# A fused two-block kernel: sums of layer 0's modulation, the end of its MLP, and block 2's second layer rearranged

## The chip, the cores and the metric

One core of one Trainium2 chip runs the whole program, a single launch. The metric is device microseconds (us), the median of the runs shown. TensorE (PE) multiplies, VectorE (DVE) and ScalarE (ACT) work on rows and evict PSUM, GpSimd (POOL) makes small powers, memsets and issues some DMAs, SyncE (SP) issues the weight loads. Every engine, and every engine's DMA queue, takes its instructions in one fixed order.

## What is computed

Block 1 is a gated residual block on 256 tokens of width 1024: a modulated RMS norm, three groups of dilated window attention, a pooling branch, and an output projection. Block 2 has two layers on the same 256 tokens and on 256 context tokens: layer 0 mixes by retention and a gated scan, layer 1 by window attention with a sink, and each has a squared-ReLU MLP. All of it is in f32.

```python
def modulation(cvec, w, b):                      # w: 1024 x 6144, two vectors: c and c_ctx
    m = jax.nn.silu(cvec) @ w + b
    return jnp.split(m[..., None, :], 6, axis=-1)   # sh1, sc1, g1, sh2, sc2, g2
...
for i in range(2):                               # block 2
    h, hc = x * (1 + sc1) + sh1, xc * (1 + csc1) + csh1
    if i == 0: y, yc = retention and gated scan of h and hc, then @ ev_w_out
    else:      q = rope(h @ w[:, :1024]); k, v from h and hc; softmax with sink; @ od_w_out
    x = layer_norm(ALPHA * x + g1 * y)
    x = layer_norm(ALPHA * x + g2 * mlp(x * (1 + sc2) + sh2))     # i == 0: the same for xc
```

## The kernel before

A large product keeps f32 accuracy by splitting each operand into two rounded halves (`hi`, `lo`) and summing three products (`mm3`, L157 to L161). A weight tile of 512 KB is loaded on SP's queue, split by ACT (`whi`, L135) and DVE (`wlo`, L136) and used by PE; four raw tiles and five split ones are kept.

Block 2's modulation is a product of two vectors with a 1024 x 6144 matrix. It is run in small steps beside other work: `fillers` is a list of generators, `fill(n)` takes n steps, and `fill_behind` takes `rate[0]` of them after each set of weights (`w_a`, `w_b`). There are two kinds. `quad` (L230) lets PE do it: each step loads 512 KB into an `mvraw` tile, and eight groups per quad, each of four column strips of 32 rows, multiply and add into one PSUM bank (L245). One quad of width 2048 gives two of the six parts. `summed` (L270) lets DVE do it: for each of eight tiles, one multiply-add per vector into an accumulator (L286, the first one L288), and at the end PE sums over the partitions with 32-column products (L292). In the kernel before, layer 0 and block 1's gate `g` are four quads, `g`, `0`, `b` and `c`, run from block 1's QKV stage up to its pooling branch at two steps per set of weights, and three per query tile inside `attention` (L569). Layer 1's six parts are `summed` inside layer 0's MLP.

Layer 0's MLP (`mlp`, L1003) ends with a group 7 in which each token tile T (order 2, 3, 0, 1) gets two products of half the width, is multiplied by its gate and added (L974, L975), measured (L357), normalised (L371), and then handed to `after0` (L1113), which makes the next layer's operand from it: eight transposes on PE (L195), eight scaled evictions on ACT (L340), a rounding and a difference on DVE (L342, L343), and, for T of 2 and 3, a copy on ACT (L1121).

Layer 1 starts with K and V of the latents (tiles 2 and 3), then K and V of the context. For each of four kv heads `rot_q` (L1162) makes 256 columns of Q: product, rotation on DVE (L1144 to L1147), a swap of partition halves by DMA on SP's queue (`swapped`), and a split in two (L1168, L1170 on DVE, L1171 on ACT). K is swapped and split likewise (L1196, L1197). `window` (L1200) runs 16 times, four per kv head: scores (L1206), masked minimum (L1213), exponential (L1215), the sink's exponential (L1217, L1218), normalising (L1223), transposes, eviction (L1227), and the product with V (L1231). After them come the output projection (`proj_out`), a layer norm (L371), `modulate` and layer 1's MLP.

The order on each engine is set when the program is built, by a scheduler that simulates a time line: it may move instructions of later code ahead. `tc.issue_after(x)` only holds the instructions written inside it behind x on x's own engine.

## Time and profile before

| | us |
|---|---|
| median of three runs (1348.94 to 1353.23) | 1349.05 |
| the profiled execution: its own time | 1356.32 |
| its span, first to last instruction | 1354.5 |

The profiled execution is 7.3 us longer than the median, and 1.8 us of it lie outside its span. Of the span TensorE is busy for 95%, VectorE for 61% and ScalarE for 43%. The stages, in us from the span's start: block 1's opening 0 to 50, QKV with quads beside it 50 to 176, its attention 176 to 262, pooling, gates and projections 262 to 375, layer 0's retention 375 to 468, its gated scan and projection to 625, its MLP to 999, layer 1's K, V and Q to 1065, its windows to about 1142, its MLP to the end. A row of a windows view gives the stretch and its length, each engine's busy time with the number of instructions, the granted TensorE clock as a share of 2.4 GHz, the DMA share and GB/s.

### The profile page before, as it was taken

The numbers are of one execution on the slowest core, as the hardware profiler recorded it, in microseconds if no ns is written. First come the engines' busy times: TensorE is split into PE (matmuls) and PEld (weight loads), VectorE is DVE, ScalarE is ACT, GpSimd is POOL, SyncE is SP. The second block draws the span as 40 slices with busy tenths as digits, with TensorE's granted clock in tenths as the row PEclk, the third lists the DMA queues.
The fourth block names the chain that finished last, engine by engine and source line by source line (L and its number), as shares of the span: only waits on it lengthen the run. The fifth ranks groups of instructions, "written<-read, shape, count | busy, mean of one in ns | idle before, by whom it ended". The sixth has DMA issues, their size and how long they took to land.

```text
span 1354.5 us, 19733 instructions
## 1 busy us (share of the span) xinstructions
PE 1286.2 (95%) x7786; PEld 1046.9 (77%) x7786; DVE 820.9 (61%) x1320; ACT 582.0 (43%) x929; POOL 85.4 (6%) x142
## 2 busy tenths in 40 slices
PE   6999998999999999998999999999989898999995
PEld 4888853699887877778878777777869676788985
DVE  4543453455745347756758666664587878466566
ACT  3433433344542263325433233323345675565652
POOL 3010021000100200001000000000020001000000
PEclk9999988999999999998999999999989899999998
DMA  9898887566622332315556566643335314365661
GB/s 321 304 300 293 274 253 233 161 198 187 184 85 78 91 86 63 125 62 171 172 156 189 182 195 211 202 140 93 93 118 149 101 32 157 118 195 177 188 177 47
DMA packets 137987, 222.22 MB, mean 164 GB/s; under 512 B 8604, under 2 KB 86052, under 8 KB 137894
## 3 DMA queue, kind: packets, MB, share of 16 engines
q1 hardware_dynamic: 131984, 206.07, 48.2%
q0 software_dynamic: 5168, 14.34, 3.7%
q8 instruction: 61, 1.00, 0.3%
q10 hardware_dynamic: 742, 0.55, 0.1%
q14 instruction: 32, 0.26, 0.1%
HBM read 217.18 MB, written 1.13 MB: 161 GB/s over the span
## 4 chain that ended last, share of the span: by engine, by line
PE 45%; DVE 5%; ACT 2%; issue 1%; DMA 1%; DVEq 0%; ACTq 0%
PE mm L159 14%; PE mm L160 13%; PE mm L161 13%; PE T L195 1%; PE O L1231 1%; DVE wlo L136 1%; PE S L1206 1%; ACT whi L135 1%; ACT hf L340 1%; DVE y L1059 1%; DMA A1t<-A1t 0%; DVE pr L1213 0%; PE O L292 0%; DVE mva L286 0%; DVE tm L974 0%
## 5 line engine op out<-in xcount | busy, mean ns | idle before, releaser
L136 DVE TENSOR_TENSOR wlo<-raw,whi 128x1024 fp32r<-128x1024 f32 x261 | 318.6, 1223 | 233.2 <-ACT whi L135 229.4
L135 ACT CAST whi<-raw 128x1024 fp32r<-128x1024 f32 x261 | 273.4, 1051 | 369.6 <-PE mm L161 198.8
L159 PE MATMUL mm<-whi,fx 128*128 128x512 f32 x384 | 154.2, 402 | 3.7 <-DVE y L1059 1.2
L160 PE MATMUL mm<-wlo,fx 128*128 128x512 f32 x384 | 152.1, 396 | 0.0
L161 PE MATMUL mm<-whi,fx 128*128 128x512 f32 x384 | 147.2, 396 | 0.0
L159 PE MATMUL mm<-A1a,whi 128*128 128x256 f32 x352 | 101.0, 287 | 0.0
L161 PE MATMUL mm<-A1a,wlo 128*128 128x256 f32 x352 | 99.3, 282 | 0.0
L160 PE MATMUL mm<-A1a,whi 128*128 128x256 f32 x352 | 99.2, 282 | 0.0
L160 PE MATMUL mm<-hBl,whi 128*128 128x512 f32 (+1 forms) x256 | 98.1, 383 | 0.0
L159 PEld LDWEIGHTS mm<-whi,fx 128*128 128x128 f32 x384 | 72.7, 189 | 27.5 <-DVE y L1059 6.8
L161 PEld LDWEIGHTS mm<-whi,fx 128*128 128x128 f32 x384 | 72.6, 189 | 17.0
L160 PEld LDWEIGHTS mm<-wlo,fx 128*128 128x128 f32 x384 | 72.7, 189 | 15.9
L159 PEld LDWEIGHTS mm<-A1a,whi 128*128 128x128 f32 x352 | 66.2, 188 | 10.0 <-issue 6.6
L286 DVE SCALAR_TENSOR_TENSOR mva<-mvraw,cst_m,mva 128x1024 f32<-128x1024 f32 x56 | 70.8, 1281 | 0.2
L111 DVE TENSOR_TENSOR fx<-f,fx 128x512 fp32r<-128x512 f32 (+1 forms) x60 | 34.0, 567 | 55.6 <-ACT fx L110 55.4
L160 PEld LDWEIGHTS mm<-A1a,whi 128*128 128x128 f32 x352 | 66.3, 188 | 0.7 <-issue 0.6
L161 PEld LDWEIGHTS mm<-A1a,wlo 128*128 128x128 f32 x352 | 66.3, 188 | 0.2 <-issue 0.2
L1059 DVE TENSOR_TENSOR y<-y,mm 128x512 f32<-128x512 f32 x72 | 47.0, 683 | 29.6 <-PE mm L161 29.5
L160 PE MATMUL mm<-hDl,whi 128*128 128x256 f32 x224 | 63.2, 282 | 0.0
L1043 ACT ACTIVATE f<-mm 128x512 f32<-128x512 f32 (+1 forms) x58 | 28.4, 490 | 78.2 <-PE mm L161 78.2
L160 PEld LDWEIGHTS mm<-hBl,whi 128*128 128x128 f32 x256 | 49.0, 191 | 10.2 <-issue 0.4
L159 PE MATMUL mm<-whi,hA 128*128 128x512 f32 x128 | 51.2, 402 | 0.0
(510 smaller groups left out, 2841.9 us busy)
## 6 DMA issues: line engine op xcount, KB each, us to landing
raw<-in_mlp_w_dram SPq DMA_DIRECT2D x128, 512.0 KB, 4.1
mvraw<-in_w_mod_dram SPq DMA_DIRECT2D x96, 512.0 KB, 4.8
raw<-in_w_in_dram SPq DMA_DIRECT2D x64, 512.0 KB, 6.2
raw<-in_ev_w_in_dram SPq DMA_DIRECT2D x25, 512.0 KB, 4.5
raw<-in_od_w_qkv_dram SPq DMA_DIRECT2D x12, 512.0 KB, 3.8
mvraw<-in_w_ada_dram SPq DMA_DIRECT2D x10, 512.0 KB, 7.6
raw<-in_w_out_dram SPq DMA_DIRECT2D x8, 512.0 KB, 3.9
raw<-in_ev_w_out_dram SPq DMA_DIRECT2D x8, 512.0 KB, 4.5
```

Source lines behind the costliest of these rows:

```text
L111: queued["split"] = nc.vector.tensor_sub(lo, src, hi.bitcast(F32)).ins
L135: nc.scalar.copy(hi, raw)
L136: queued["lo"] = nc.vector.tensor_sub(lo, raw, hi.bitcast(F32)).ins
L159: nc.tensor.matmul(o, lh, rh, start=first, stop=False)
L160: nc.tensor.matmul(o, lh, rl, start=False, stop=False)
L161: nc.tensor.matmul(o, ll, rh, start=False, stop=last)
L195: nc.tensor.transpose(o, i, ident[:n, :n])
L286: nc.vector.scalar_tensor_tensor(acc, raw, stat[:, k, m:m + 1], acc, op0=ALU.mult, op1=ALU.add)
L340: nc.scalar.activation(hf[:, i, :], pt[:, i * P:(i + 1) * P], AF.Identity, scale=A[:, c + i:c + i + 1], bias=B[:, c + i:c + i + 1])
L1043: nc.scalar.activation(f, o, AF.Relu)
L1059: nc.vector.tensor_add(y[:, T, hs], y[:, T, hs], o)
L1206: nc.tensor.matmul(sp[e], Q2[:, kv % 2, e, c % 2, qs], KK[:, part, kv // 2, kv % 2, :], start=part == 0, stop=part == 1)
```

## The change

Block 1's gate and layer 0's parts sh1, sc1, sc2 and g2 (`ga2_0`) are no longer quads but `summed`: `g` and sh1 beside QKV (one step per set of weights, two from the third group on), sc1 beside the pooling branch and the gates, sc2 and g2 inside retention (`fill(2)` and `fill(1)` placed by hand, the rest at its end). Only the quad `b` (g1 and sh2) stays, and it runs inside `attention`, after `while fillers: fill(1)` has emptied the list. `mvraw` has four buffers in block 1, and the sums in retention have three of their own.

At the end of an MLP the products of tiles 2 and 3 come first, one tile after the other (`issue_after(ends[-2])`), each tile is normalised as soon as it is whole, the next layer's operand of tile 2 is made before the products of tiles 0 and 1, and that of tile 3 between their two halves; the ACT copies of tiles 2 and 3 go behind the last eviction.

In layer 1 the Q of kv head n + 1 is made behind the scores of the first window of head n, no longer ahead of its own; the swapped halves of Q and K are copied by DMA from the split ones, on POOL's queue, and not split again; the sink's exponential takes its sum as ACT's bias; ACT normalises the second head of a pair; the last kv head goes query tile by query tile, and the residual's two tiles are renewed after head 1 and head 2.

```diff
-            nc.tensor.matmul(o, ll, rh, start=False, stop=last)
+            queued["mm"] = nc.tensor.matmul(o, ll, rh, start=False, stop=last).ins
...
-                    raw = pool.tile([P, 1024], F32, tag="mvraw", name="mvraw", bufs=3)
+                    raw = pool.tile([P, 1024], F32, tag="mvraw", name="mvraw", bufs=4)
                     nc.sync.dma_start(raw, wv[:, k, col + 1024 * h:col + 1024 * h + 1024])
...
-        def summed(pool, res, key, w, col, b, stat, vecs, rows=False):
+        def summed(pool, res, key, w, col, b, stat, vecs, rows=False, name="", accs=None):
...
-            accs = [pool.tile([P, D], F32, tag="mva", name="mva", bufs=2) for _ in range(vecs)]
+            if not isinstance(accs, list):
+                accs = [pool.tile([P, D], F32, tag=accs or "mva", name="mva", bufs=2) for _ in range(vecs)]
...
-                raw = pool.tile([P, D], F32, tag="mvraw", name="mvraw", bufs=3)
+                raw = pool.tile([P, D], F32, tag="mvraw", name="mvraw", bufs=4 if pool is p1t else 3)
                 nc.sync.dma_start(raw, wv[:, k, col:col + D])
...
-                    nc.scalar.activation(hf[:, i, :], pt[:, i * P:(i + 1) * P], AF.Identity, scale=A[:, c + i:c + i + 1], bias=B[:, c + i:c + i + 1])
+                    queued["hf"] = nc.scalar.activation(hf[:, i, :], pt[:, i * P:(i + 1) * P], AF.Identity, scale=A[:, c + i:c + i + 1],
+                                                        bias=B[:, c + i:c + i + 1]).ins
...
-        fillers.append(quad(p1t, p1t, "g", a["w_ada"][0], 2048, a["b_ada"][0], cst_a, 1, 256, "g"))
...
-        fillers.append(quadcols("0", 0))
-        fillers.append(quadcols("b", 2048, "b0"))
-        fillers.append(quadcols("c", 4096, "c0"))
-        rate[0] = 2
+        fillers.append(summed(p1t, None, "g", wa, 2 * D, ba, cst_a, 1, True, accs="PT"))
+        fillers.append(summed(p1t, m0, "sh1", w_mod[0], 0, b_mod[0], cst_m, 2, name="m0", accs="PT"))
+        rate[0] = 1
 
         qT, kT = [], []
         vall = A0a[:, 0:3].rearrange("p g (t n) -> p g t n", t=2)
         for g in range(3):
+            if g == 2:
+                rate[0] = 2
             at = (h1a, h1a, h0a)[g], (0, 2, 0)[g]
             q_, k_ = part(at[0], at[1], 1), part(at[0], at[1] + 1, 1)
             for i in range(2):
...
+        while fillers:
+            fill(1)
+        fillers.append(quadcols("b", 2 * D, "b0"))
...
+        fillers.append(summed(p1t, m0, "sc1", w_mod[0], D, b_mod[0], cst_m, 2, name="m0", accs="PT"))
...
-        yp_h = p1t.tile([P, 4, S], F32R, tag="PT", name="yp_h")
+        yp_h = p1t.tile([P, 4, S], F32R, tag="sq", name="yp_h")
...
+        sums = slot("qkb", "mva", [P, 2, D])
+        fillers.append(summed(p2r, m0, "sc2", w_mod[0], 4 * D, b_mod[0], cst_m, 2, name="m0", accs=[sums[:, 0], sums[:, 1]]))
+        fillers.append(summed(p2r, None, "ga2_0", w_mod[0], 5 * D, b_mod[0], cst_m, 2, True, accs=[sums[:, 0], sums[:, 1]]))
+        rate[0] = 0
...
+            fill(2)
...
-                        nc.vector.tensor_mul(sm_[h][:, i, :], sps[e][:, i, :], W[:, h, P * (1 - i):P * (1 - i) + S])
+                        last = nc.vector.tensor_mul(sm_[h][:, i, :], sps[e][:, i, :], W[:, h, P * (1 - i):P * (1 - i) + S]).ins
+                with tc.issue_after(last):
...
+                with tc.issue_after(queued["head"]):
+                    fill(1)
...
+        fill(100)
...
-                last = Ts[len(Ts) // 2:] + Ts[:len(Ts) // 2] if len(Ts) > 2 else Ts
-                for i, T in enumerate(last):
-                    st = None
+                sts, ends = {}, []
+
+                def products(T, half):
+
+                    with tc.issue_after(ends[-2]) if len(ends) > 1 else nullcontext():
+                        o = gemm_b(ws[half], fh, fl, Ts.index(T))
+                    ends.append(queued["mm"])
+                    gate_add(y, o, T, slice(512 * half, 512 * half + 512))
+
+                def normed(T):
+                    norm(y[:, T, :], ln_stats(y[:, T, :], 1, ln_stats(y[:, T, :], 0)))
+
+                for T in Ts[-2:]:
                     for half in range(2):
-                        gate_add(y, gemm_b(ws[half], fh, fl, Ts.index(T)), T, slice(512 * half, 512 * half + 512))
-                        st = ln_stats(y[:, T, :], half, st)
-                    norm(y[:, T, :], st)
-                    if i:
-                        after(last[i - 1])
+                        products(T, half)
+                    normed(T)
+                if len(Ts) > 2:
+                    after(2)
+                    for T in Ts[:2]:
+                        products(T, 0)
+                    after(3)
+                    for T in Ts[:2]:
+                        products(T, 1)
+                    with tc.issue_after(queued["mod"]):
+                        normed(0)
+                        normed(1)
+                    after(0)
 
 
...
-            if T > 1:
-                nc.scalar.copy(resid(T), y0[:, T, :])
+            if T == 3:
+                with tc.issue_after(queued["hf"]):
+                    for t in (2, 3):
+                        nc.scalar.copy(resid(t), y0[:, t, :])
...
-        qs_ = xc.rearrange("p t (b e n) -> p t b e n", b=2, n=S)
+        qs_ = xc[:, 0].rearrange("p (b e n) -> p b e n", b=2, n=S)
...
-        def swapped(dst, src):
-
-            for _, nat, oth in sides:
-                nc.sync.dma_start(dst[nat], src[oth])
-
...
-            q, sw = qs_[:, 0, b], qs_[:, 1, b]
+            q = qs_[:, b]
             rot(q, gemm_a(wq, 256 * kv, hx), 2, 0.125)
-            swapped(sw, q)
             r = main.tile([P, 2, S], F32R, tag="t2", name="qr", bufs=4)
-            nc.vector.tensor_copy(r, q)
+            nc.scalar.copy(r, q)
             for e, nat, oth in sides:
+                nc.gpsimd.dma_start(Q2[oth, b, e], r[nat])
                 nc.vector.tensor_sub(Q2[nat, b, e], q[nat], r[nat].bitcast(F32))
-                nc.scalar.copy(Q2[oth, b, e], sw[oth])
 
 
         kT = gc.rearrange("p (j n) -> p j n", j=2)
...
-            swapped(kS[:, :, hs], kT[:, :, hs])
             for e, nat, oth in sides:
-                for sl, src in ((nat, kT), (oth, kS)):
-                    nc.scalar.copy(KK[sl, 0, :, e, hs], src[sl, :, hs])
-                    nc.vector.tensor_sub(KK[sl, 1, :, e, hs], src[sl, :, hs], KK[sl, 0, :, e, hs].bitcast(F32))
+                nc.scalar.copy(KK[nat, 0, :, e, hs], kT[nat, :, hs])
+                nc.vector.tensor_sub(KK[nat, 1, :, e, hs], kT[nat, :, hs], KK[nat, 0, :, e, hs].bitcast(F32))
+                nc.gpsimd.dma_start(KK[oth, :, :, e, hs], KK[nat, :, :, e, hs])
         to_rows(gx, "ga1", 0, 0)
...
+                nc.scalar.activation(es[:, e:e + 1], m[:, e:e + 1], AF.Exp, bias=sink[:, 0, 2 * c + e:2 * c + e + 1])
                 prs.append(pr_)
-            nc.vector.tensor_add(es, sink[:, 0, 2 * c:2 * c + 2], m)
-            nc.scalar.activation(es, es, AF.Exp)
...
-                nc.vector.tensor_scalar_mul(prs[e], prs[e], den[:, e:e + 1])
+                if e:
+                    nc.scalar.activation(prs[e], prs[e], AF.Copy, scale=den[:, e:e + 1])
+                else:
+                    nc.vector.tensor_scalar_mul(prs[e], prs[e], den[:, e:e + 1])
...
+        lnr = ln_rows([p4.tile([P, D], F32, tag="lnr", name="lnrr", bufs=2) for _ in range(2)], (0, 1))
         for kv in range(4):
-            if kv:
-                rot_q(kv)
-            for c in (2 * kv, 2 * kv + 1):
-                for qt in range(2):
-                    window(kv, c, qt)
-            if kv == 1:
-                lnr = ln_rows([p4.tile([P, D], F32, tag=t, name=t + "r") for t in ("kS", "lnr")], (0, 1))
-            if kv == 2:
+            cs = (2 * kv, 2 * kv + 1)
+            for n, (c, qt) in enumerate([(c, qt) for c in cs for qt in range(2)] if kv < 3 else [(c, qt) for qt in range(2) for c in cs]):
+                window(kv, c, qt)
+                if n == 0 and kv < 3:
+                    with tc.issue_after(queued["qk"]):
+                        rot_q(kv + 1)
+            if kv in (1, 2):
                 with tc.issue_after(queued["split"]):
-                    for T in (2, 3):
-                        new_resid(T, resid(T), lnr)
+                    new_resid(kv + 1, resid(kv + 1), lnr)
 
         r1 = slot("A0", "r1", [P, 4, D])
         cx = mod_cols("x0b", 4, 8, mod1["sc2"], mod1["sh2"], 0)
```

## Rows read from the trace of the kernel before

**Rows 1.** The page's first part: busy us, share of the span, instructions, by engine
```profile
PE 1286.2 (95%) x7786; PEld 1046.9 (77%) x7786; DVE 820.9 (61%) x1320; ACT 582.0 (43%) x929; POOL 85.4 (6%) x142
```

**Rows 2.** Windows of five stages, columns as told above
```profile
50.00:176.00 126.00, 126.00 (x921) 105.38 (x924) 55.58 (x63) 50.54 (x57) 8.16 (x14) 1.00 0.88 292
176.00:262.00 86.00, 76.79 (x419) 36.72 (x412) 33.15 (x100) 27.97 (x63) 15.56 (x23) 0.90 0.69 212
375.00:468.00 93.00, 92.90 (x521) 76.21 (x520) 43.18 (x88) 29.72 (x48) 12.04 (x18) 1.00 0.26 76
1006.00:1065.00 59.00, 52.88 (x412) 51.15 (x411) 47.50 (x88) 33.07 (x62) 3.86 (x3) 0.96 0.45 133
1065.00:1142.00 77.00, 73.88 (x532) 56.45 (x532) 62.88 (x176) 51.82 (x129) 2.87 (x5) 0.96 0.23 71
```

**Rows 3.** Windows of the quads' products alone (L245), four stretches: PE, PEld, clock, DMA
```profile
50.00:108.00 58.00, 5.10 (x64) 1.68 (x64) 1.00 0.87 289
108.00:176.00 68.00, 8.70 (x68) 1.41 (x72) 1.00 0.89 294
176.00:262.00 86.00, 30.67 (x112) 3.88 (x104) 0.90 0.69 212
262.00:300.00 38.00, 2.13 (x16) 0.31 (x16) 1.00 0.66 207
```

**Rows 4.** Groups by line, TensorE, 176 to 262: busy, mean ns | idle before, releaser
```profile
L245 PE MATMUL O<-mvraw,cst_m 128*32 128x512 f32 x112 | 30.8, 674 | 8.8 <-DMA mvraw<-in_w_mod_dram 8.7
```

**Rows 5.** Time line of TensorE: start, us, instruction; one quad step, one closing sum
```profile
122.07 1.07 PE L245 MATMUL O<-mvraw,cst_m 128*32 128x512 f32 x8
...
697.50 1.07 PE L292 MATMUL O<-mva,sel 128*32 128x256 f32 x16
```

**Rows 6.** Groups by line and form, whole span, VectorE: the multiply-adds of the sums
```profile
L286 DVE SCALAR_TENSOR_TENSOR mva<-mvraw,cst_m,mva 128x1024 f32<-128x1024 f32 x56 | 70.8, 1281 | 0.2
L288 DVE TENSOR_SCALAR mva<-mvraw,cst_m 128x1024 f32<-128x1024 f32 x8 | 5.9, 749 | 1.3 <-PE O L292 1.3
```

**Rows 7.** Time line of VectorE and TensorE, 982 to 1147; idle before in brackets
```profile
982.54 1.89 DVE L974 TENSOR_TENSOR tm<-mm,A1t 128x512 f32<-128x512 f32 x3 [4.57 <-PE mm L161]
...
1005.62 0.80 PE L159 MATMUL mm<-hCh,whi 128*128 128x256 f32 x2 [5.34 <-DVE hCh L342]
...
1060.01 0.73 PE L1206 MATMUL S<-KK,Q 128*128 128x512 f32 x2 [1.45 <-DVE m L1213]
...
1065.23 1.97 PE L195 MATMUL T<-ident,pr 128*128 128x128 f32 x8 [4.49 <-DVE pr L1223]
...
1146.50 0.79 PE L159 MATMUL mm<-whi,hDh 128*128 128x512 f32 x1 [2.72 <-DVE hDh L342]
```

**Rows 8.** Groups by line, ScalarE, the stage of the windows (1065 to 1136)
```profile
L1215 ACT ACTIVATE pr<-pr,m 128x512 f32<-128x512 f32 x28 | 20.3, 725 | 1.8 <-DVE m L1213 1.7
L1227 ACT COPY PT<-T 128x512 f32<-128x512 f32 x32 | 17.5, 586 | 12.2 <-PE T L195 12.2
L1215 ACT ACTIVATION_READ_ACCUMULATOR pr<-pr,m 128x1 f32 x28 | 5.4, 192 | 0.0
L135 ACT CAST whi<-raw 128x1024 fp32r<-128x1024 f32 x3 | 3.1, 1046 | 0.5 <-PE mm L161 0.3
L1218 ACT ACTIVATE es<-es 128x2 f32<-128x2 f32 x14 | 2.8, 198 | 1.1 <-DVE es L1217 1.1
L1171 ACT CAST Q<-A1t 64x512 fp32r<-64x512 f32 x4 | 2.5, 618 | 0.9 <-PE S L1206 0.8
```

**Rows 9.** Groups by line, VectorE, the same stretch
```profile
L1223 DVE TENSOR_SCALAR pr<-pr,den 128x512 f32<-128x512 f32 x32 | 14.2, 485 | 0.2
```

**Rows 10.** Groups by line and form, whole span, ScalarE, in place on 128 x 512
```profile
L1044 ACT ACTIVATE f<-f 128x512 f32<-128x512 f32 x32 | 20.2, 633 | 1.0
```

**Rows 11.** DMA issues: queue, count, KB each, median us from issue to landing
```profile
kS<-A1t SPq DMA_DIRECT2D x4, 128.0 KB, 2.5
...
msk<-cst_msk_dram POOLq DMA_DIRECT2D x1, 128.0 KB, 2.7
```

More of the change, by code (lines that the diff above doesn't have):

```diff
@@ L1 @@
 import math
-from contextlib import ExitStack
+from contextlib import ExitStack, nullcontext
 import numpy as np
@@ L655, in body @@
             nc.sync.dma_start(xc[:, t, :], a["ctx_2"][0, t * P:(t + 1) * P, :])
[L656 to L657 removed]
+        cc = mod_cols("c0a", None, None, m0["sc1"], m0["sh1"], 1)
+        cx = mod_cols("x0a", 1, None, m0["sc1"], m0["sh1"], 0)
         for t in range(2):
@@ L736, in head_norm @@
                 if first:
-                    nc.vector.tensor_scalar_mul(y[:, h, :], o[:, h, :], rs[:, h:h + 1])
+                    queued["head"] = nc.vector.tensor_scalar_mul(y[:, h, :], o[:, h, :], rs[:, h:h + 1]).ins
                 else:
```

19 lines of the change are left out of this document (8 added, 11 removed).

## Prediction

> **What bounds the kernel now.** I read the page's first part, then the stages, then in each touched stage what stands before the late instructions. TensorE is busy for 95% of the span, VectorE for 61%, ScalarE for 43% [rows 1]: time comes back where TensorE loses work, an idle stretch, or a stretch at the lower clock. By stage [rows 2]: from 50 to 176 it is busy for all of 126 us at the full granted clock, so work taken out shortens the stage one for one. From 176 to 262, block 1's attention, it is busy for 76.8 of 86 us at a mean clock of 0.90: work, idle time and clock all count. In retention, 375 to 468, it is full again, and VectorE has 50 of 93 us free. From 1006 to 1065 and from 1065 to 1142, layer 1's projections and windows, 6.1 and 3.1 us are idle and the clock is 0.96 in both; as it has two levels, 1.2 and 2.4 GHz, 0.96 means 8% at the lower one, which costs 4% of the stretch, 2.4 and 3.1 us.
>
> **The change part by part.** Durations are of the profiled execution, 1356.3 us in all, 1354.5 of it the span. It stands 7.3 us above the median of 1349.05; I take the sum off 1356.3 and scale by 1349.05/1356.32 = 0.9946.
>
> *Gate and sh1 beside QKV.* The quads `g` and `0` leave: 5.10 and 8.70 us of TensorE [rows 3]. What comes is a closing product per sum. One of two vectors, 16 records, takes 1.07 us [rows 5]; `g` has one vector, so 0.54 + 1.07 = 1.6 us. Net 12.2 us gained. On VectorE come 24 multiply-adds, three first ones of 0.749 and 21 of 1.281 us [rows 6], 29.1 us. Cover: VectorE is busy for 55.6 of 126 us [rows 2]; 84.7 of 114 would still be free time. The tight place is the third group, with two steps per set of weights. One set is 48 products at 126 us/921 = 0.137, 6.6 us of TensorE; VectorE's own share is 44% of that, 2.9, and two steps of sh1 add 4 x 1.281 = 5.1: 8.0 us per 6.6. It falls 1.4 us behind per set, 5.7 over the four sets that sh1 needs. Queued behind a sum are the differences `wlo`, for which TensorE waits; but five split tiles, two and a half sets, are ready ahead, 16 us. I take 0; without that cover 5.7.
>
> *Attention.* Before, `b` and `c` run here: 112 + 16 records for 32.8 us [rows 3], and TensorE idles 8.8 us for their loads [rows 4]. Only `b` is left: half of both, so 16.4 + 4.4 us go, and sc1's closing product adds 1.1: 19.7 us. A step costs 1.07 us where its eight records run together [rows 5], but 30.67/14 = 2.19 us each in attention; if `b` ran at 1.07 and waited for no load, the gain would be 32.8 - 8.6 + 8.8 - 1.1 = 31.9. The other end: TensorE's own work here is 46.1 of 86 us, the rest of each query tile is a chain of minimum, exponential and eviction which the quads fill; if that chain surfaces, I bound the gain by 6, under a third of 19.7. Projections of the pooling branch can move up into the gaps, since SP's queue holds 16 loads of `c` less ahead of their weights. I take 16. The sums of sc1, 16 multiply-adds, fall in the full projections behind attention, one step per set, inside the cover reckoned above.
>
> *sc2 and g2 in retention.* Two closing products, 2.1 us. 32 multiply-adds, 4 x 0.749 + 28 x 1.281 = 38.9 us, into 93 us where VectorE has 43.2 [rows 2]: 82 of 93. That is room, but little: behind each step of 2.6 us wait the masked scores and the norms, for which the value products wait, and six steps are left for the end, 15 us, before which the slot of the sums can't take the scan's Q and K. On SP's queue 16 loads join where DMA is 26% busy. On POOL's, a memset and small transfers per sum stand ahead of the norms' powers. Exposed: nothing, to a quarter of it, 10 us. I take 2.5, near the low end since TensorE's own projections are there to be moved into gaps. Together 4.6 us lost (2.1 to 12.1).
>
> *The end of layer 0's MLP.* Three products end together before VectorE gets the first (1.89 us for three, after 4.57 idle), and TensorE then idles 5.34 us for the operand of tile 3 [rows 7]; the clock loss of the next stage is 2.4. With one tile's products at a time the first add starts two products earlier, ScalarE's two residual copies go behind the evictions, and two product pairs lie behind each operand's making. Up to 7.7 us. VectorE has gates, statistics, roundings and `wlo` all in these 20 us, in order, so I take 4 (0 to 7.7). In layer 1's MLP the same order moves only the last rows: 0.
>
> *Layer 1.* TensorE idles 1.45 and 4.49 us before the first windows [rows 7], when VectorE rotates three heads' Q beside the first minima; that moves into the windows. Three projections, 144 products at 52.88/412 = 0.128, 18.5 us, now fill the windows' gaps instead of standing ahead. At the end TensorE idles 2.72 us for tile 2's operand [rows 7], which the last head's new order makes one or two windows earlier. With the clock's 3.1 us the most is 11.8 us. Against it: ScalarE. Per window it gains a scaling in place and one exponential of a column. The scaling is not in the trace; nearest are 0.633 (square in place) [rows 10], 0.586 and 0.725 [rows 8]; I take the first, plus 0.198. Over 1065 to 1142: 51.8 + 16 x 0.831 + six weight tiles at 1.046 + six evictions of Q at about 0.59 - four `Q` casts at 0.618 [rows 8] = 51.8 + 13.3 + 6.3 + 3.5 - 2.5 = 72.4 us. TensorE has 73.9 - 3.1 + 18.5 = 89.3. ScalarE is at 81%, so TensorE stays the bound, with longer chains per window. VectorE loses 16 scalings of 0.485 [rows 9], 7.8 us. The copies: before, swapped halves landed in 2.5 us on SP's queue, ahead of the split; now behind it on POOL's, where 128 KB took 2.7 [rows 11]. K's last copy stands ahead of the first scores, with V's projection (48 x 0.128 = 6.1 us) as cover; no other projection can go there now, since Q is held behind the scores. 0 to 5 us late; the copies of the later heads have four windows each. I take 9 for the layer (-6 to 11.8).
>
> At one place the Trainium skill speaks against the change. The rows show no difference by queue, 2.7 on POOL's against 2.5 us on SP's for 128 KB [rows 11]. The Trainium skill, "SBUF — State Buffer", section "SBUF: two separate sides", says that GpSimd can't write the descriptors of a DMA on its queue while VectorE runs a copy or a scaling in its two-port mode; such a transfer then appears stalled. By that rule each copy would be late by the VectorE instruction under way; what it would make here is the third rival.
>
> **Sum.** 12.2 + 16 - 4.6 + 4 + 9 = 36.6 us. 1356.3 - 36.6 = 1319.7, scaled 1313. All good ends together give 12.2 + 31.9 - 2.1 + 7.7 + 11.8 = 61.5, scaled 1288; all bad ends together 12.2 - 5.7 + 6 - 12.1 + 0 - 6 = -5.6, slower than before; both need five steps to agree.
>
> **The rivals.** *Attention's own chain* takes the place of the quads: its gain is 6, the sum 26.6, the time 1323. For it: the mean clock of 0.90 and short runs of products there [rows 2]. Against: TensorE had nothing to wait for but loads [rows 4]. *ScalarE bounds the windows*: layer 1 loses 6 instead of gaining 9, the sum is 21.6, the time 1328. For it: 72 us of ScalarE in chains. Against: TensorE's 89. *The port*: 12 copies, each late by one VectorE scaling of 0.485 [rows 9], are 5.8 us if all lie on the path: 1319. For it stands only the rule of the Trainium skill named above; against it the landing times. *VectorE becomes the bound*, the one on the other side: the 72 multiply-adds, 9 x 0.749 + 63 x 1.281 = 87.4 us, delay `wlo` and the scores in order, and TensorE waits. It decides from the point where VectorE's share of a stage reaches all of it, the third group or retention (88% by the sum). To be slower than before by 0.3%, 36.6 + 4.1 us more than the 2.5 taken must come out into the open, half of all sums; at 48 us the time is 1360. Against it: VectorE has free time by the sum in each of the three places, and the 56 multiply-adds of layer 1's sums ran with 0.2 us idle before them [rows 6], so their loads came in time. *All good ends*, half-way or more: 1295. That the change does not do what it says: the quads are out of the program, so TensorE's work falls in any case; only the order is the scheduler's.
>
> **How the numbers follow.** My forecast 0.48, attention's chain 0.17, ScalarE 0.15, the port 0.05, VectorE 0.06, good ends 0.09. 1313 is the likeliest. The range 1296 to 1336 takes in the first four with one more step at its bad end; it leaves out VectorE's case, the joint worst of the first two rivals with retention's 10 us (0.04, about 1345), and half of the good ends. 0.3% of 1349, 4 us, is about what a measurement can tell from no change: faster 0.90; same 0.04, the joint worst; slower 0.06.
>
> **What would show it.** 46 us of L245 become about 14, with the rest of them in attention; attention ends some 25 us earlier, with TensorE idle there under 9 us, else the first rival. The retention stage grows by under 5 us with VectorE near 88%; waits of products for `wlo`, or of the scan's Q and K for the sums, would be VectorE's case. The 5.34, 4.49 and 2.72 us are gone or under half. ScalarE's share of the windows stays under TensorE's. The forecast is wrong if TensorE's new idle time, summed, is over 20 us, or if the clock falls in stages where it was full.

## The result: 0.55% slower

The changed kernel takes 1359.38 us, the median of four runs (1357.39 to 1361.57), the kernel before 1349.34 (1348.94 to 1353.23): a ratio of 1.0055, 95% interval 1.0028 to 1.0082. Forecast were 1313 us and a range of 1296 to 1336.

The profiled executions, 1357.39 and 1356.32 us, are nearer to each other than the medians, since that of before lies 7 us above its median; so up to 7 us of what stretches of before take can be that execution's own. What follows compares stretches between marks that both programs have.

### The profile page after: what moved, and what is told of

It is laid out like the page before. It is cut to its first block, busy times and chain, and to the rows that moved or that the text cites. A ratio compares the mean times of both kernels' runs of the same rounds, so it can differ in the third digit from the quotient of the medians.

```text
span 1355.5 us, 19590 instructions
## 1 busy us (share of the span) xinstructions
PE 1273.0 (94%) x7664; PEld 1049.6 (77%) x7664; DVE 887.2 (65%) x1355; ACT 591.6 (44%) x953; POOL 91.1 (7%) x160
## 5 line engine op out<-in xcount | busy, mean ns | idle before, releaser
L288 DVE SCALAR_TENSOR_TENSOR mva<-mvraw,cst_m,mva 128x1024 f32<-128x1024 f32 x112 | 140.2, 1278 | 0.2
L160 PE MATMUL mm<-hBl,whi 128*128 128x512 f32 (+1 forms) x256 | 97.6, 382 | 0.0
L160 PE MATMUL mm<-wlo,hA 128*128 128x512 f32 x128 | 51.2, 400 | 0.0
```

The source lines that it names most:

```text
L160: nc.tensor.matmul(o, lh, rl, start=False, stop=False)
L288: nc.vector.scalar_tensor_tensor(acc, raw, stat[:, k, m:m + 1], acc, op0=ALU.mult, op1=ALU.add)
```

## The profile after

The engines' line of the page, which answers to [rows 1]:

```profile
PE 1273.0 (94%) x7664; PEld 1049.6 (77%) x7664; DVE 887.2 (65%) x1355; ACT 591.6 (44%) x953; POOL 91.1 (7%) x160
```

TensorE's busy time fell by 13 us, VectorE's rose by 66, and the span did not fall. The quads' products (L245) alone fell by 33.0 us, from 46.6 to 13.6, and the closing products of the sums rose by 6.6, from 4.9 to 11.5; so all other products together take some 13 us longer than before. TensorE lost elsewhere what it was spared. Windows of after, columns as in [rows 2]: QKV, attention, and then, from the last product of block 1's gates on, retention in two stretches, the end of its sums, and projections and the scan in two stretches.

```profile
50.00:163.40 113.40, 113.40 (x816) 101.81 (x815) 81.35 (x87) 50.02 (x56) 8.53 (x15) 1.00 0.86 288
163.40:235.00 71.60, 62.78 (x363) 36.84 (x355) 32.20 (x101) 26.81 (x61) 15.03 (x23) 0.90 0.56 180
...
337.50:392.00 54.50, 52.88 (x334) 46.86 (x333) 30.92 (x53) 24.82 (x44) 5.04 (x9) 1.00 0.49 155
392.00:450.00 58.00, 57.76 (x326) 44.85 (x324) 49.91 (x85) 12.67 (x20) 7.49 (x11) 1.00 0.53 162
450.00:462.00 12.00, 4.49 (x22) 2.28 (x23) 8.28 (x9) 2.97 (x5) 2.88 (x6) 0.66 0.49 134
462.00:525.00 63.00, 63.00 (x342) 47.57 (x340) 31.60 (x58) 29.43 (x41) 3.99 (x7) 0.98 0.26 74
525.00:565.50 40.50, 35.22 (x233) 25.81 (x232) 28.97 (x74) 14.59 (x24) 4.20 (x5) 0.84 0.31 104
```

And windows of the kernel before, from the same mark to the same end (363.5 to 569.4):

```profile
363.50:412.00 48.50, 48.40 (x311) 43.41 (x310) 25.20 (x42) 23.70 (x43) 4.14 (x6) 1.00 0.35 103
412.00:470.00 58.00, 58.00 (x315) 45.78 (x313) 25.11 (x60) 13.80 (x22) 12.04 (x18) 1.00 0.30 92
470.00:530.00 60.00, 60.00 (x342) 44.14 (x340) 33.31 (x62) 31.52 (x43) 0.00 (x0) 1.00 0.28 80
530.00:569.40 39.40, 37.74 (x256) 29.35 (x254) 28.41 (x67) 15.62 (x26) 3.57 (x4) 1.00 0.24 79
```

Block 1 went as forecast. From 50 to attention's first minimum, and from there to 2 us behind its last products, the kernel before has these two rows for after's first two:

```profile
50.00:177.20 127.20, 127.20 (x929) 105.62 (x928) 56.74 (x65) 51.02 (x57) 8.80 (x15) 1.00 0.87 290
177.20:262.00 84.80, 75.59 (x411) 36.49 (x408) 31.98 (x100) 27.49 (x62) 14.93 (x23) 0.90 0.70 215
```

QKV is 13.8 us shorter, 1.9 of it an earlier start (its first product stands at 54.6 instead of 56.5), and attention 13.2; 1.0 is lost again behind them. By the last product of `mg` the changed kernel is 26.0 us ahead:

```profile
L159 PE MATMUL mm<-whi,mg x32: 390/393/483, 340.9 to 363.5; 128*128 128x512 f32 x32
...
L159 PE MATMUL mm<-whi,hA x128: 387/393/505, 377.0 to 560.7; 128*128 128x512 f32 x128
...
L159 PE MATMUL mm<-whi,yH x64: 388/394/795, 569.4 to 619.1; 128*128 128x512 f32 x64
```

```profile
L159 PE MATMUL mm<-whi,mg x32: 390/393/482, 314.9 to 337.5; 128*128 128x512 f32 x32
...
L159 PE MATMUL mm<-whi,hA x128: 388/393/583, 350.5 to 542.4; 128*128 128x512 f32 x128
...
L159 PE MATMUL mm<-whi,yH x64: 388/394/793, 565.5 to 615.7; 128*128 128x512 f32 x64
```

(Each row: count, shortest, median and longest duration in ns, first and last start; the first three rows are of before, the last three of after.) By the first product of `yH` the lead is 3.9 us: 569.4 against 565.5. The 205.9 us between these two marks became 228.0, so 22.1 us are lost there. The windows say how: idle time of TensorE is 14.6 us of the 228.0 against 1.8 before, and the clock, full in all of before's four rows, is 0.66 from 450 to 462 and 0.84 from 525 to 565.5. From 450 to 462 that is 7.5 us idle, and of the 4.5 busy ones up to 2.2 lost by the clock; from 525 to 565.5 it is 3.6 us more idle than at the same place before, and 16% of 40.5, up to 6.5 us, by the clock. With 1.6 us idle at the start and the sums' own products, 2 to 3, these make up the loss (23 to 24 us with both clock terms at their most). The timeline of after shows the first of these two places (start, duration, instruction, idle time before it and what ended it):

```profile
437.05 2.47 DVE L288 SCALAR_TENSOR_TENSOR mva<-mvraw,cst_m,mva 128x1024 f32<-128x1024 f32 x2
...
453.48 3.67 DVE L288 SCALAR_TENSOR_TENSOR mva<-mvraw,cst_m,mva 128x1024 f32<-128x1024 f32 x3
...
449.36 0.40 PE L161 MATMUL mm<-hA,wlo 128*128 128x512 f32 x1
...
456.11 2.19 PE L294 MATMUL O<-mva,sel 128*32 128x256 f32 x16 [6.35 <-DVE mva L288]
...
458.41 2.44 ACT L872 ACTIVATE qkb<-mm 64x512 f32<-64x512 f32 x4 [7.80 <-PE O L294]
...
460.26 0.63 PE L160 MATMUL mm<-hA,whi 128*128 128x512 f32 x1
```

From 437.05 to 457.15 VectorE runs without a gap, and only sums (`mva`) and `wlo`; the last sum's closing product stands in TensorE's order 6.35 us for it. Behind it come the scan's Q and K (`qkb`, which takes the sums' slot): ScalarE sits idle for 7.80 us before their eviction. And behind it comes `lrT`, from which the scan's decays are made; VectorE copies it right after the last sum's addition:

```profile
458.37 0.42 DVE L295 TENSOR_TENSOR mvb<-O,mvb 128x256 f32<-128x256 f32 x1 [1.21 <-PE O L294]
458.82 0.70 DVE L824 COPY lrT<-mm 32x512 f32<-32x512 f32 x1
```

In the program `fill(100)`, which ends the sums, stands ahead of `lrT`. The scan's first product (L883) follows this copy by 38.2 us, at 497.0; in the kernel before by 38.0, 457.8 to 495.8. Counted from the last product of `mg`, the copy stands at 121.3 us instead of 94.3, and the scan starts at 159.5 instead of 132.3: 27.2 us later. It is 5.1 us shorter then, 68.5 instead of 73.6, since fewer projections are left to run beside it, and the two make the 22.1 us. The second place is the rows of `hA` above: the last projection that can stand beside the scan starts at 542.4, 23.1 us ahead of the scan's end; before it was 8.7 us. Such projections had been moved up beside the sums.

In layer 1 the changed kernel stands again. Timeline ahead of the first scores, and how long the two copies of the first Q took from issue to landing:

```profile
1031.51 0.68 DVE L1184 TENSOR_TENSOR A1t<-A1t,rots 128x512 f32<-128x512 f32 x1
...
1032.22 0.62 ACT L1199 CAST qr<-A1t 128x512 fp32r<-128x512 f32 x1 [0.73 <-DVE A1t L1184]
1033.13 1.06 POOL L1201 DMA_DIRECT2D Q<-qr  x2 [8.51 <-ACT qr L1199]
...
1038.62 0.77 PE L1235 MATMUL S<-KK,Q 128*128 128x512 f32 x1 [8.49 <-DMA Q<-qr]
```

```profile
DMA to landing us min/median/max: 5.4/5.7/6.0
```

Rotation, rounding on ScalarE, the issue on GpSimd's queue and 5.5 us to the scores: TensorE idles 8.49 us for the first copy of Q. Windows up to the first scores, and from there to the last product of `proj_out`, in after and then in before (1007 and 1014 are not the same place in the program):

```profile
1007.00:1038.60 31.60, 20.97 (x159) 20.09 (x158) 19.47 (x30) 16.88 (x33) 3.55 (x6) 0.87 0.57 141
1038.60:1145.70 107.10, 98.47 (x693) 77.22 (x694) 72.07 (x174) 77.65 (x182) 5.75 (x11) 0.96 0.22 63
```

```profile
1014.00:1047.80 33.80, 33.39 (x279) 32.83 (x277) 25.13 (x41) 20.42 (x39) 0.57 (x1) 1.00 0.48 139
1047.80:1140.50 92.70, 84.27 (x610) 66.30 (x610) 77.64 (x206) 61.94 (x148) 2.31 (x4) 0.96 0.27 81
```

Ahead of the scores TensorE has 10.6 us idle at a clock of 0.87, where before it had 0.4 idle at full clock: the projections of the later heads, which filled that stretch, now stand behind the scores. The second stretch holds 693 products instead of 610 and is 14.4 us longer. Between marks that both have, the first product of `hCh` and the first of layer 1's MLP (1005.6 and 1146.5 before, 994.3 and 1147.6 after), the layer takes 153.3 us instead of 140.9: 12.4 lost.

## Experiments

Theory: two separate losses, the sums in retention (which end late, and then a scan without cover) and layer 1's first Q without cover. Rivals are in the expectations. Ratios are to the kernel before in the same session, with 95% intervals; kernels of different sessions are compared by ratio. First four kernels that take one or both losses away.

**a_l1old.** Layer 1 from `qs_` to the loop over the heads as before:

```diff
-            q = qs_[:, b]
+            q, sw = qs_[:, 0, b], qs_[:, 1, b]
...
+            swapped(sw, q)
...
-                nc.gpsimd.dma_start(Q2[oth, b, e], r[nat])
```

> The changed kernel with layer 1 (Q, K, windows) put back as in the kernel before; the rest of the change stays. Theory: the changed kernel loses its time in two places, in retention with the scan behind it, and at the head of layer 1, where TensorE stands 8.5 us for the first copy of Q and then runs at a lower clock; from the first scores to the first product of layer 1's MLP the changed kernel lost about 10 us. Put back, it takes 1359.4 - 10 = about 1349 us, and the wait of 8.5 us is gone. Rival, layer 1's loss is not its own but made by the new order at the end of layer 0's MLP, which stays: then about 1358.

Measured: 1345.14 us, ratio 0.9954 (0.9914 to 0.9993). Against 1.0055 that is 1.0%, 13.6 us, a little more than expected; layer 1's change is a loss by itself.

**b_nosums.**

```diff
-        fillers.append(summed(p2r, m0, "sc2", w_mod[0], 4 * D, b_mod[0], cst_m, 2, name="m0", accs=[sums[:, 0], sums[:, 1]]))
-        fillers.append(summed(p2r, None, "ga2_0", w_mod[0], 5 * D, b_mod[0], cst_m, 2, True, accs=[sums[:, 0], sums[:, 1]]))
...
-        cc = mod_cols("c0b", 2, 6, m0["sc2"], m0["b"][:, 8:16], 1)
+        cc = mod_cols("c0b", 2, 6, m0["sc1"], m0["b"][:, 8:16], 1)
```

> The changed kernel without the two sums in retention: sc1's columns stand for sc2's and the rows of g1 for those of g2, so 32 multiply-adds, two closing products and 16 loads are left out. Theory: the sums made VectorE late, the scheduler put projections of the scan ahead to fill TensorE, TensorE stood 7.7 us at the end of the sums, and the scan behind lost its cover: some 21 us of the lead of 25 go there. Without the sums: 1359.4 - 21 = about 1338, and the last projection of hA ends as close to the scan's end as before. Rival, only the visible wait at the end of the sums and the products themselves (7.7 + 3) are the sums' price, the rest of the lead is lost by the scan whatever stands ahead of it: about 1349.

Measured: 1340.26 us, 0.9901 (0.9871 to 0.9932), 20.8 us under the changed kernel by the ratios. The rival's 1349 falls. From the last product of `mg`, `lrT` stands at 95.7 us and the scan starts 37.9 later; the last projection of `hA` is again 8.7 us ahead of the scan's end.

**c_moved.**

```diff
         fillers.append(summed(p1t, m0, "sc1", w_mod[0], D, b_mod[0], cst_m, 2, name="m0", accs="PT"))
+        fillers.append(summed(p1t, m0, "sc2", w_mod[0], 4 * D, b_mod[0], cst_m, 2, name="m0", accs="PT"))
...
+        fillers.append(summed(pm, None, "ga2_0", w_mod[0], 5 * D, b_mod[0], cst_m, 2, True))
         for i, key in enumerate(("sh1", "sc1", "ga1", "sh2", "sc2", "ga2")):
```

> The changed kernel with the same sums at other places: sc2 behind sc1 beside block 1's gates (one step per set of weights), g2 first in the list of layer 0's MLP. Theory: both places have VectorE free and a full TensorE, so it takes what the kernel without these sums takes, plus the closing products, 2 to 3 us: about 1341. Rival, a place for 16 more multiply-adds beside the gates costs as much as in retention, because VectorE is needed there in order too: about 1350.

(The two `fillers` lines of retention go, as in b_nosums, and the rows of g2 are spread later in the MLP.) Measured: 1339.40 us, 0.9903 (0.9871 to 0.9934). The same sums cost nothing that these runs can tell at other places: it was the place. It was not VectorE's share by itself, which is higher beside the gates than it was in retention:

```profile
270.00:310.00 40.00, 40.00 (x343) 38.90 (x342) 37.46 (x42) 16.51 (x20) 2.01 (x3) 1.00 0.86 287
```

VectorE is busy for 94% of these 40 us, TensorE for all of them at full clock.

**d_moved_l1old.** Both edits together.

> The moved sums and layer 1 put back as before, together. Theory: the two losses are in different places and add up: 1341 - 10 = about 1331, faster than the kernel before by 18. Rival, the gain of the one hides the other (TensorE's clock, or the loads of weights, take part of it back): 1340 or more.

Measured: 1331.28 us, 0.9836 (0.9794 to 0.9877), 29.6 us under the changed kernel. The two edits by themselves gave 13.6 and 20.5, together 34.1; within the error the losses add up.

The next four ask what in layer 1 costs, and price the other two parts.

**e_cover.** On c_moved:

```diff
+        rot_q(1)
         for kv in range(4):
...
-                if n == 0 and kv < 3:
+                if n == 0 and 0 < kv < 3:
```

> The kernel with the moved sums (1339.4 us, ratio to the kernel before 0.990) and layer 1 as changed, except that the second head's Q is projected ahead of the first window and not held behind its scores; the heads after it stay spread. Theory: the 8.1 us before the first scores are the copy of the first Q (128 KB, 4.7 us from issue to landing) with no product left to stand beside it; 48 products at 0.128, 6.1 us, now do, so about 7 us come back: 1332, ratio 0.985, and the wait on the copy falls under 3 us. Rival, the copies are late by the queue they are on and the head's clock stays low: the wait moves behind the projection and 1337 or more remain.

Measured: 1326.55 us, 0.9796 (0.9766 to 0.9826), the fastest of all, 14.4 us better than c_moved by the ratios, twice what was expected. Its waits of TensorE ahead of the windows (us in total, times, longest), and its windows up to the first scores and to the end of `proj_out`:

```profile
PE S L1235 <- DMA Q<-qr: 2.1, 2, 1.9
```

```profile
984.00:1016.20 32.20, 28.14 (x233) 27.28 (x231) 24.37 (x39) 20.35 (x38) 4.20 (x7) 1.00 0.53 138
1016.20:1111.80 95.60, 92.32 (x645) 70.33 (x646) 69.81 (x173) 74.00 (x179) 5.74 (x11) 0.96 0.24 71
```

The wait for Q is 1.9 us, the clock ahead of the scores full, idle time there 4.1 us instead of the 10.6 of the changed kernel. Where the 48 products now stand they cost nothing: from the first product of `hCh` to the first scores it is 42.0 us, in c_moved 42.4. From there to the first product of layer 1's MLP it is 97.5 instead of 109.2, 6.1 of it those products and 4.5 less idle time of TensorE (4.1 instead of 8.6).

**f_spq.** On c_moved:

```diff
-                nc.gpsimd.dma_start(Q2[oth, b, e], r[nat])
+                nc.sync.dma_start(Q2[oth, b, e].bitcast(F32), r[nat].bitcast(F32))
...
-                nc.gpsimd.dma_start(KK[oth, :, :, e, hs], KK[nat, :, :, e, hs])
+                nc.sync.dma_start(KK[oth, :, :, e, hs].bitcast(F32), KK[nat, :, :, e, hs].bitcast(F32))
```

> The kernel with the moved sums and layer 1 as changed, the copies of Q and K issued by SyncE on its own queue instead of GpSimd's. Rival to the lack of cover, the third rival of the prediction: GpSimd's queue makes them late; then they land in some 2.5 us as the swaps of the kernel before did, and 2 to 4 us come back, 1336. Theory, the lack of cover: the copy's way is rounding, issue and 128 KB beside weight loads on either queue; less than 2 us change, 1338 to 1341, and TensorE still stands 6 us or more for it.

Measured: 1339.95 us, 0.9900 (0.9864 to 0.9935): nothing. The landing of the two copies of the first Q, in c_moved and then here, and TensorE's wait here:

```profile
DMA to landing us min/median/max: 4.8/5.1/5.3
```

```profile
DMA to landing us min/median/max: 4.7/4.7/4.7
```

```profile
PE S L1235 <- DMA Q<-qr: 7.8, 1, 7.8
```

The copies that the first scores wait for took 4.7 us on SyncE's queue and 4.8 and 5.3 on GpSimd's, and the scores waited 7.8 us instead of 8.1. The queue is not the cause; the missing cover is, as e_cover shows.

**g_mlpend_old.** On d_moved_l1old, the end of both MLPs as before:

```diff
-                for T in Ts[-2:]:
...
                     for half in range(2):
-                        products(T, half)
-                    normed(T)
...
+                    if i:
+                        after(last[i - 1])
```

> The kernel with the moved sums and layer 1 as before (1331.3 us, ratio 0.984), with the end of both MLPs also put back as before. Theory: the new order at the end of layer 0's MLP is worth the 4 us of the forecast (0 to 7.7): 1335, and the wait of 5.3 us for tile 3's operand is back. Rival, TensorE is late by the same stretch further on, because VectorE has the same work: within 1 us of 1331.

Measured: 1335.08 us, 0.9862 (0.9834 to 0.9889). 3.5 us by the ratios, in the theory's direction; the two intervals overlap, so by itself it is inconclusive.

**h_window_new.** On d_moved_l1old:

```diff
+                nc.scalar.activation(es[:, e:e + 1], m[:, e:e + 1], AF.Exp, bias=sink[:, 0, 2 * c + e:2 * c + e + 1])
...
+                if e:
+                    nc.scalar.activation(prs[e], prs[e], AF.Copy, scale=den[:, e:e + 1])
```

> The kernel with the moved sums and layer 1 as before, with the body of the window alone as changed: ScalarE scales the second head of a pair and takes the sink's sum as its bias. Theory: VectorE loses 16 scalings of 0.485 us, ScalarE gains 13 us in the windows, and neither bounds them: within 2 us of 1331. Rival, ScalarE's longer chain per window is a part of the loss of layer 1 (the second rival of the prediction): 1335 or more.

Measured: 1331.03 us, 0.9835 (0.9805 to 0.9864). No difference; ScalarE's longer chain does not bound the windows in the old order of Q. In the new order, where TensorE has more to do in them, it was not tried alone.

The next four test the causes further: the cover alone, half the sums, the MLP's end beside the cover, and which part of a sum costs.

**i_cover_only.** The edit of e_cover on the changed kernel.

> The changed kernel with one edit: the second head's Q is projected ahead of the first window; both sums stay in retention. Theory: the two losses are separate and add up, so the cover gives here what it gave beside the moved sums, 1339.4 - 1326.6 = 13 us: 1359.4 - 13 = 1346, ratio to the kernel before 0.997. Rival, the gain there needed the earlier start that the moved sums gave: 1352 or more.

Measured: 1347.24 us, 0.9957 (0.9937 to 0.9978): this one edit turns the slower kernel into a slightly faster one, 13.2 us by the ratios. It is also where a_l1old is (0.9954): beside the two sums in retention, layer 1 as changed with the cover and layer 1 as before take the same time.

**j_one_sum.** On e_cover, sc2 back in retention:

```diff
-        fillers.append(summed(p1t, m0, "sc2", w_mod[0], 4 * D, b_mod[0], cst_m, 2, name="m0", accs="PT"))
...
+        sums = slot("qkb", "mva", [P, 2, D])
+        fillers.append(summed(p2r, m0, "sc2", w_mod[0], 4 * D, b_mod[0], cst_m, 2, name="m0", accs=[sums[:, 0], sums[:, 1]]))
```

> The kernel with cover and moved sums (1326.6 us, ratio 0.980), but sc2 summed in retention again; g2 stays in layer 0's MLP. Theory: retention has room on VectorE for one sum, 43.2 + 2 x 0.749 + 14 x 1.281 = 62.6 of 93 us, and none is left for its end: at most 3 us more, 1330, no wait of TensorE at the sum's end, and the last projection of hA ends within 6 us of the scan's end. Rival, any sum there makes VectorE late for the masked scores and pulls the scan's projections ahead: half the price of two, 9 us, 1336.

Measured: 1329.56 us, 0.9812 (0.9785 to 0.9839). Within the error of e_cover. Windows of retention's second stretch and of the scan's end:

```profile
388.00:445.00 57.00, 57.00 (x325) 44.26 (x324) 43.16 (x83) 13.27 (x21) 11.24 (x18) 1.00 0.40 120
...
505.00:548.00 43.00, 42.10 (x269) 31.94 (x267) 30.14 (x73) 15.41 (x25) 3.50 (x5) 1.00 0.19 60
```

TensorE has no idle time in this stretch of retention and the clock stays full; `lrT` stands at 97.6 us after the last product of `mg`, 1.9 later than without sums: one sum fits.

**k_cover_mlpend_old.** The edit of g_mlpend_old on e_cover.

> The kernel with cover and moved sums, with the end of both MLPs as before. Theory: the new order there is worth some 4 us (1335.1 against 1331.3 in the pair without the cover): 1330.5. Rival, it only moves the wait: within 1.5 us of 1326.6.

Measured: 1337.90 us, 0.9875 (0.9844 to 0.9907), against 0.9796: 10.7 us, more than the theory's 4, and the intervals are apart. TensorE's waits from 930 to 1040, first in this kernel, then in the changed one:

```profile
PE mm L159 <- DVE hCh L345: 5.5, 2, 5.3
```

```profile
PE mm L159 <- DVE hCh L345: 1.2, 1, 1.2
```

The 5.3 us for the operand of tile 3 are [rows 7]'s 5.34; the new order leaves 1.2. The profiled executions lie 16.1 us apart, 8.3 of it between the first product of `yH` and the first scores (480.0 us against 471.7), where the edit acts, and 4.3 ahead of that, where the edit touches nothing; so a part of the 10.7 can be the executions' own. The rest of it stays open.

**l_narrow.** On the changed kernel, for the two sums of retention:

```diff
+                nn = 32 if k and key in ("sc2", "ga2_0") and name + key in ("m0sc2", "ga2_0") else D
...
-                        nc.vector.scalar_tensor_tensor(acc, raw, stat[:, k, m:m + 1], acc, op0=ALU.mult, op1=ALU.add)
+                        nc.vector.scalar_tensor_tensor(acc[:, 0:nn], raw[:, 0:nn], stat[:, k, m:m + 1], acc[:, 0:nn], op0=ALU.mult, op1=ALU.add)
```

> The changed kernel; of the two sums in retention all but the first multiply-add of each vector work on 32 of 1024 columns, which leaves that work out (28 multiply-adds of 1.28 us become short ones); loads, closing products and their order in the program stay. Theory: the price of the sums is VectorE's time, which delays the masked scores and stands in the way of the end; without it 1359.4 - 16 = 1343. Rival, it is the 16 loads on SyncE's queue, GpSimd's small transfers and the closing products in TensorE's order: 1354 or more.

Measured: 1343.27 us, 0.9920 (0.9894 to 0.9946), 18.2 us under the changed kernel, as the theory had it. Its windows of the same stage, which answer to the last five of after:

```profile
340.80:392.00 51.20, 49.58 (x309) 44.71 (x308) 26.21 (x44) 23.28 (x42) 5.04 (x9) 0.97 0.43 138
392.00:450.00 58.00, 58.00 (x331) 45.49 (x330) 30.52 (x93) 12.69 (x20) 6.95 (x11) 1.00 0.50 169
450.00:505.00 55.00, 53.62 (x259) 39.53 (x259) 23.82 (x37) 26.40 (x34) 6.88 (x12) 1.00 0.43 131
505.00:559.20 54.20, 49.19 (x360) 38.12 (x356) 38.39 (x98) 22.08 (x37) 3.50 (x4) 0.94 0.21 78
```

TensorE no longer stands at the sums' end. But between the two marks its profiled execution takes 218.4 us, against 207.3 in e_cover and 228.0 in the changed kernel, and the scan's end is again bare: the last projection of `hA` starts at 534.3, 24.9 us ahead, with 5.0 us idle and a clock of 0.94 in the last row. The profiled executions of the two lie 11.8 us apart, 9.6 of it in this stage. The sums end only 6.7 us earlier than in the changed kernel (112.9 us after the last product of `mg` instead of 119.6), `lrT` stands at 116.7, and the scan starts at 154.5, still 22.2 later than in the kernel before. So VectorE's time was not all of it, and two more kernels ask whether the slot is, which the sums take from the scan's Q and K.

**m_own_tiles.** On the changed kernel:

```diff
-        sums = slot("qkb", "mva", [P, 2, D])
+        sums = vx[:, 0:4].rearrange("p (m u) n -> p m (u n)", m=2)
```

> The changed kernel with the accumulators of retention's two sums in the slot that the scan's V takes, no longer in that of its Q and K; all work stays. Theory A, the slot: Q and K no longer wait for the end of the sums, the scan starts some 15 us earlier, projections are left to stand beside its end, and the half of the loss that l_narrow's stage still had comes back: 1359.4 - 10 = 1349, ratio 0.998. Theory B, VectorE's time alone: the scan is late because the sums are, whoever holds the slot: within 3 us of 1359, ratio 1.005.

Measured: 1362.34 us, 1.0069 (1.0045 to 1.0093): theory A falls. (The profiled execution, 1372.85 us, is 10.5 above this median, so its waits are on the long side.) TensorE's longest wait of the stage, ScalarE's, and the rows of `hA` and `yH`:

```profile
PE O L294 <- DVE vx L288: 15.8, 1, 15.8
ACT vx L860 <- PE O L294: 16.5, 1, 16.5
```

```profile
L159 PE MATMUL mm<-whi,hA x128: 388/393/796, 359.2 to 576.7; 128*128 128x512 f32 x128
...
L159 PE MATMUL mm<-whi,yH x64: 388/394/628, 579.7 to 631.8; 128*128 128x512 f32 x64
```

The last projection of `hA` now starts 3.0 us ahead of the scan's end, which is covered, and the wait of 6.35 us at the sums' end has become 15.8. But the edit did not set the scan free from the sums. Its V is evicted beside them in the changed kernel, from 68.9 us after the last product of `mg` on; here it waits for their end, until 111.6. Q and K are evicted from 130.9 on, later than the 120.9 of the changed kernel and not earlier, and `lrT` still follows the last sum, at 113.2. So the wait was passed on from Q and K to V, and this kernel is no clean test of theory A. That projections can hide one of the two places and not both fits its rows; it was not shown by itself.

**n_own_narrow.** The same edit on l_narrow.

> The same edit together with the short multiply-adds of l_narrow (all but the first of each vector on 32 of 1024 columns, which leaves that work out). Theory A: with neither VectorE's time nor the slot, what is left of the sums costs their closing products, 2 to 3 us over the kernel without sums (1340.3): 1342, and the stage from the last gate product to the first of the scan's output projection is under 211 us instead of 218.4. Theory B: nothing but what l_narrow has, 1343, with the stage as there, 218.

Measured: 1356.26 us, 1.0022 (1.0004 to 1.0040), worse than both theories; the edit alone costs l_narrow 13.8 us. TensorE's longest wait and ScalarE's for V, and then that of SyncE's queue for the sums' buffers between 390 and 470:

```profile
PE O L295 <- DVE vx L289: 9.9, 1, 9.9
ACT vx L861 <- PE O L295: 10.6, 1, 10.6
```

```profile
SPq L284 <- DVE vx L289: 34.5, 8, 9.9
```

With the sums' work on VectorE almost gone they still end late, 106.9 us after the last product of `mg`: their steps stand behind the norms in program order, the load of a step waits until one of three buffers is read (34.5 us of waiting on SyncE's queue, 24.9 in l_narrow), and then VectorE waits for the load (6.4, and 5.9 in l_narrow). So the sums' late end has two causes, VectorE's time and this chain of loads, steps and buffers; these runs don't share it out between them. The chain is not what n_own_narrow loses against l_narrow, though: there the sums end later still, at 112.9, and TensorE never waits for them. What differs is V, which as in m_own_tiles waits for the sums' end. And in both kernels `lrT` follows the last sum as before, so the scan starts 153.9 and 148.3 us after the mark; no kernel here moves `lrT` alone.

## Why the prediction was wrong, step by step

**What bounds the kernel**: right. TensorE's lost time, idle and at the lower clock, is what decides in every trace read here.

**QKV and attention**: right in mechanism, a little large. Forecast 28.2 us, read off the marks 24.1 (26.0, less the 1.9 of the opening). L245 is down to 13.6 us, as named ("about 14"). QKV gave 11.9 of its 12.2. Attention gave 13.2 inside its stage; of the forecast 16 some was to come from projections moved up. TensorE is idle there for 8.8 us, just under the 9 that were named as the bound for the first rival.

**sc2 and g2 in retention**: the first failed step. It was put at -4.6, at worst -12.1, and is -22.1 by the marks, 20.8 by b_nosums. The count of the work was right, but 88% was never the share of that stage: over the 93 us that answer to it VectorE is busy for 64.8, 70%, since the last steps run past its end; in the fullest 58 us it is at 49.9, 86%. Two things were wrong. I reckoned VectorE's share over the whole stage, while the six steps left for the end made it full from 437 to 457; I named their 15 us and the slot behind them, but not `lrT`, which also stands behind them and starts the scan 27.2 us late, and then priced the exposure at 2.5 "since TensorE's own projections are there to be moved into gaps". These projections are the same that cover the scan. They were spent beside the sums, and the scan then ran its end bare, with 5.3 us idle and a clock of 0.84, near half of the loss as the windows have it. A cover was counted twice. m_own_tiles shows the same cover spent the other way round, scan covered and sums bare, though with V's wait added. The rival "VectorE becomes the bound" (0.06) had the place, the scan's Q and K behind the sums, but my point for it, a share of all of the stage, was too late: what decides is when the last sum ends and what is queued behind it; beside the gates 94% cost nothing (c_moved). That its 1360 is the time measured is chance: it put 48 us down to the sums, which cost 22, and nothing to layer 1. That the late end is VectorE's time holds in part (l_narrow gains 18.2 us, m_own_tiles to n_own_narrow 6.3); besides it there is the sums' own chain of loads and buffers, which I had looked at only as DMA share. With one sum nothing is lost (j_one_sum), nor with both at other places (c_moved).

**The end of layer 0's MLP**: right in direction. Forecast 4; 3.5 with layer 1 as before, 10.7 beside the cover.

**Layer 1**: the second failed step. Forecast +9, measured -13.6 (a_l1old) and -9.0 (d_moved_l1old against c_moved). TensorE was to be the bound, with 89 us of work to ScalarE's 72, and so it is (98 and 78 in the second stretch); the loss begins ahead of it. The -6 of my range had no sum behind it. I had written that K's last copy has V's projection as its only cover and that "no other projection can go there now", and priced K's copy alone. The first Q's chain, rotation, rounding and a copy with 5.5 us from issue to scores, runs behind it, with nothing left: 8.5 us idle, then products at the lower clock (a granted clock of 0.56 from 1038.6 to 1045). The 2.7 us that I took for a copy on GpSimd's queue were a mask's load from DRAM; the first two copies of Q took 5.4 and 6.0. e_cover gives that cover back and nothing else. What layer 1's change is then worth is not settled: 5.4 us against layer 1 as before with the sums moved (0.9796 against 0.9836, intervals that overlap), nothing with them in retention (i_cover_only 0.9957, a_l1old 0.9954). The 9 is not shown.

**ScalarE as the bound**: h_window_new speaks against it, in the old order of Q. **The port**: f_spq took the copies off GpSimd's queue and gained nothing; the first two landed 0.1 and 0.6 us earlier than in c_moved. The Trainium skill, "SBUF — State Buffer", section "SBUF: two separate sides", says that GpSimd can't write the descriptors of such a transfer while VectorE runs in a two-port mode. If that is behind these 0.6 us no run here shows; it is not the 8.1 us that TensorE waits.

**The sum** with the measured terms: 24.1 - 22.1 + 3.5 - 9.0 to 13.6 is 3.5 to 8.1 us lost; the ratio gives 7.4. Of the 44 us between forecast and result, 17.5 are retention, 18 to 23 layer 1, 4 block 1.

## What to carry to other kernels

Independent work that hides a wait can be spent once: before pricing a wait at nothing because other products can move there, look where those products stand now and what they hide in that place. Reckon an engine's room up to the point where someone waits for the last of its work, not over the stage, and list everything that the program puts behind that last work: here the slot of Q and K, and the first copy of the scan. A hold that spreads work (`issue_after`) also forbids its use as cover at the start of the stretch; keep one piece outside the hold, as e_cover does, which with the moved sums is 2.0% faster than the kernel before.

## What I had not expected of the hardware

One idle stretch costs beyond itself. After TensorE stood 6.35 us at 449.76, the closing products and the next ones ran at the lower of its two levels: the granted clock averages 0.66 from 450 to 462 and is 0.50 from 456 to 462, and products take 0.63 us that took 0.40 before, at full clock (rows above, 460.26 and 449.36); ahead of the first scores of layer 1, 10.6 idle us went with a clock of 0.87. In the scan's end short products with 5.3 us of idle time between them went at 0.84, and the same end with long products among them, in e_cover, at 1.00:

```profile
505.00:544.50 39.50, 37.85 (x257) 29.32 (x253) 28.44 (x67) 15.59 (x26) 3.57 (x4) 1.00 0.23 80
```
